# Scores of two attentions: the 64-row matmul with key lo runs over 128 rows, and key lo is loaded into both halves

## The chip, the cores and the metric

The kernel runs on one core of a Trainium2 chip. The metric is the device time of one execution in microseconds (us), median of three runs; lower is better. The engines are TensorE (PE in the rows, its weight loads PEld), VectorE (DVE), ScalarE (ACT), GpSimd (POOL) and SyncE (SP), which issues the DMAs.

## The reference, cut to what matters

Two blocks of two layers work on 512 tokens of 1024 features. Two of the mixers are attentions, and each computes scores with heads of 64 features:

```python
p1 = jax.nn.softmax(jnp.einsum('bqhd,bkhd->bhqk', q1, k1).astype(jnp.float32) * scale, axis=-1)
p2 = jax.nn.softmax(jnp.einsum('bqhd,bkhd->bhqk', q2, k2).astype(jnp.float32) * scale, axis=-1)
p = (p1 - lam * p2).astype(v.dtype)
...
s = jnp.einsum('bqgrd,bkgd->bgrqk', qg, k).astype(jnp.float32) * (d ** -0.5)
...
scores = jnp.einsum("bpnqhd,bpnkhd->bpnhqk", qb, kw) * (1.0 / math.sqrt(dh))
...
scores = jnp.where(valid[:, None], scores + bias, NEG_INF)
```

The first three lines are the differential heads of the first attention, the fourth its grouped heads (queries of 512 tokens, keys of 256 context tokens and of the 512), and the last two the second attention, with 16 heads, three dilated windows each and a bias by distance.

All of it is in fp32.

## The kernel before

Every fp32 operand of a product is split into two parts, hi and lo, in the matmul type fp32r; a general product takes three matmuls, hi by hi, hi by lo and lo by hi (`mm`, L187 to L192). A score uses that a head has only 64 features: `stack` (L707) puts q hi of head i of a pair into its own 64 rows of a tile and q lo into the other 64, and `load_twice` (L715) puts k hi into both halves of a tile. One matmul over 128 rows (L730) then gives (q hi + q lo) by k hi. A second one over the head's 64 rows (L731) adds q hi by k lo. Its k lo comes from `load_one` (L722), which loads a pair's two heads into one tile.

The first attention (`attention1`) has 48 blocks of 128 queries: four differential heads in two pairs, with two scores a block, and eight grouped heads with one, so 64 scores; a score has 768 keys, as 512 and 256 columns, and so two L730 and two L731. The second (`attention2`) has 64 blocks, eight pairs of heads with eight blocks each. A block has three scores, one of 512 keys (into bank `s0`) and two of 128 (into `s1`), so three L730 and three L731. Scores run two blocks ahead of the products with v. Between them `q_steps` weaves in the query products of the next pair (bank `side`). A block's softmax goes over DVE (L1414, L1417, L1426), ACT (L1422) and POOL, is transposed on PE (L825), split by ACT and DVE (L145, L148), and multiplied with v (L841).

PE takes its instructions in the written order inside the attentions; the other engines and the DMA issues are ordered by a scheduler at build time. All loads stand in one queue, SP's. `shift` and `accs` are two tiles of the layer norm (`ln_begin`, L498), in use until the norm ahead of the second attention is done and again in the norm behind it.

Of the kernel before, what the change touches and what calls it, by code (L numbers as in the profile page):

```python
# [15 lines left out]
PSUM = bass.MemoryType.PSUM  # L16
# [12 lines left out]
# PE takes its products in the order in which they are written  # L29
# [23 lines left out]
class Head:  # L53
    # the first products of the part behind a norm: the tokens that it ends first come first
# [27 lines left out]
class QueryHead(ColumnHead):  # L82
    # done before the attention's own banks are there
# [9 lines left out]
class TokenHead(Head):  # L93
    # 128 tokens by 512 columns to a bank, chunks of two row tiles
# [11 lines left out]
class Net:  # L106
# [26 lines left out]
    def side(self):  # L133
        # the bank of what is woven between the blocks of an attention
        return self.t(self.ps, [P, 512], F32, "side", 1)
# [37 lines left out]
    def chunk(self, name, idx, nb, w=128, k0=0):  # L173
# [4 lines left out]
        with ExitStack() as es:  # L178
            # behind the norm that the products before this one wait for
            if self.gated:  # L180
                self.gated -= 1
                for g in self.gate:
                    es.enter_context(self.tc.issue_after(g.ins))
            self.split(src, hi, lo)
# [14 lines left out]
    def out_gemm(self, names, base, xs, update, finish=None, tail=4, lead=0, loads=None, done=(0, 0)):  # L199
        # a product that adds to x; its last column tiles by halves of the tokens, for the norm behind it  # L200
        # done = (m, k): the first m column tiles have their first k row tiles in x already
# [8 lines left out]
        # the first column tiles at once, row tile by row tile: the last of them may still be in the making  # L210
# [14 lines left out]
        # x is updated behind the products of the next column tile  # L225
# [102 lines left out]
    def affine_split(self, t, a, b, hi, lo, R=None):  # L328
        # hi + lo = t * R * a + b
# [10 lines left out]
    def setup(self, es):  # L340
# [18 lines left out]
        # two regions of 16 tiles: what a product reads, and what is made from it  # L359
        self.rp = self.pool(es, "regions")  # L360

# [1 line left out]
    def ada_raw(self, pool, l, m, tag, bufs):  # L363
        # 128 columns of the modulation's weights, columns on the partitions
# [10 lines left out]
    def ada_start(self):  # L375
        # silu(c) and silu(c_ctx) along the rows of all partitions
# [11 lines left out]
    def ada_first(self, k):  # L388
        # shift and scale of row tile k of layer 0's mixer, for both conditions; the second sum is left to a later call
# [25 lines left out]
    def gain(self, l, which):  # L415
        # norm gain times (1 + scale)
# [5 lines left out]
    def ada_rest(self, l, j, engine=None):  # L422
        # column blocks of 512, 12 to a layer; summed over the partitions with a later call
# [54 lines left out]
    def rms_end(self, sl, a, b):  # L478
        # h = x * rsqrt(mean x^2 + eps) * a + b
# [23 lines left out]
    def ln_update(self, m, ps, scale, sl):  # L503
        # the sums run over x less the mean of its first 256 features: no more than 4 times the variance
# [116 lines left out]
    def gained(self, pool, ps, gain, tag, bufs, g=None, s=None):  # L621
        # ps * gain and ps ^ 2, out of PSUM
# [8 lines left out]
    def mean_sq(self, v, s, dim, eps, rhs=None):  # L631
        # column sums of s, as means and eps, into v
# [4 lines left out]
    def scaled_steps(self, g, y, gain=None):  # L637
        # g by the rows of y: [128 tokens, tiles of 128 tokens * groups of rows]
# [17 lines left out]
    def q_steps(self, next_chunk, dst, slot=None):  # L656
        # a column tile of queries, in steps; dst takes the rows for the scores, or what the norm goes on with
# [11 lines left out]
    def q_norm_steps(self, next_chunk, dsts, slots, v, key=None):  # L669
        # two column tiles of queries with their norms, and the keys'  # L670
# [18 lines left out]
    def diff_norm_steps(self, ots, zs):  # L689
        # the norms of the differential heads; zs has the sums of the first softmax  # L690
# [16 lines left out]
    def stack(self, q, src, view=lambda z: z):  # L707
        # head i of a pair as 128 rows: hi where src has it, lo in the other half
# [6 lines left out]
    def load_twice(self, pool, src, i, tag, bufs):  # L715
        # the rows of head i, in both halves
# [10 lines left out]
    def score(self, out, q, kk, kl, i, qs, ks):  # L727
        # (q hi + q lo) k hi + q hi k lo
        r = slice(64 * i, 64 * i + 64)
        self.nc.tensor.matmul(out=out, lhsT=q[i][:, qs], rhs=kk[:, ks], start=True, stop=False)  # L730
        self.nc.tensor.matmul(out=out, lhsT=q[i][r, qs], rhs=kl[r, ks], start=False, stop=True)  # L731
# [33 lines left out]
    def v_store(self, pool, vt, slot):  # L765
# [3 lines left out]
        # hi and lo of a head side by side, in the other order for the second one  # L769
# [6 lines left out]
    def v_all(self, pool):  # L776
        # the values of the four differential heads, tokens on the partitions: context, then latents
# [18 lines left out]
    def scores(self, q, k, i, qt):  # L796
        # [128 queries, 768 keys] of head i of a pair
# [5 lines left out]
    def softmax(self, pool, s):  # L803
        # exp(s - max) and its sums; what follows the maximum with a second call
# [12 lines left out]
    def p_t(self, e, pt, q, nk):  # L817
        # transposes P and splits it
# [17 lines left out]
    def pv_stacked(self, ps, v, pt, nk, i, out, parts=1):  # L836
        # (v hi + v lo) (p hi + p lo): those with v hi in the rows of head i, those with v lo in the others
# [11 lines left out]
    def diff_weights(self, ap, q, k, i, qt, zs, fill):  # L849
        # (softmax 1 - lam softmax 2) times the sum of softmax 1, which the norm of the head takes out  # L850
# [15 lines left out]
    def gqa_weights(self, ap, q, k, i, qt):  # L866
        # query heads m and m + 4 share a tile: the rows of head m + 4 i are those of key head i
# [8 lines left out]
    def lam(self):  # L876
        # misc[:, 0] = -(exp(lq1.lk1) - exp(lq2.lk2) + lam_init), misc[:, 1] = subln (1 - lam_init)
# [14 lines left out]
    def attention1_start(self, es, hc):  # L892
        # the first modulation and norm, and the queries of the differential heads and two tiles of keys with them:
        # row tile by row tile, as they come
# [5 lines left out]
        with self.tc.manual_schedule(engines=PE_ORDER):  # L900
# [10 lines left out]
            # products that take the row tiles as they come: queries, then keys  # L911
# [777 lines left out]
```

## Time and profile before

| what | value |
|---|---|
| median of 3 runs | 3589.59 us (3586.48 to 3591.5) |
| span of the profiled execution | 3579.7 us, 9.9 us below that median |
| PE busy | 3422.9 us, 96% of the span |
| weight loads (PEld) busy | 2843.5 us, 79% |
| DVE, ACT, POOL busy | 58%, 40%, 11% |
| granted clock of PE, mean | 0.976 of full speed |
| first attention, from its first score | about 188 to 446 us |
| second attention | about 2826 to 3138 us |

The span runs from the first to the last instruction of one execution that the profiler recorded; the profile gives no other time for that execution, and what lies around the span is taken as the difference to the median. Matmuls are pipelined and their recorded ends overlap, so what one costs is read from start to start.

### The profile page before, as it was taken

The page shows a single profiled execution, that of the slowest core. Times are in us where ns is not written, and L with a number is a line of the kernel's source. Part 1 is how long each engine was busy: PE and PEld are TensorE (multiplying, and loading weights), DVE is VectorE, ACT ScalarE, POOL GpSimd, SP SyncE. Part 2 cuts the span into 40 slices and gives each one's busy share as a digit, 9 for nine tenths or more (in the row PEclk, how much of TensorE's full clock was granted, in tenths as well). Part 3 has the DMA queues.
Part 4 walks back from the last instruction along what each step waited for, and adds up shares of the span by engine and source line. Part 5 has one row for each costly group of instructions (what it writes and reads, how often), then busy time and mean ns, then how long its engine had stood idle before and what let it go on. Part 6 is the DMA issues. An engine that isn't in the chain of part 4 may idle for free.

```text
span 3579.7 us, 43200 instructions
## 1 busy us (share of the span) xinstructions
PE 3422.9 (96%) x16646; PEld 2843.5 (79%) x16646; DVE 2068.3 (58%) x3471; ACT 1415.8 (40%) x2145; POOL 392.5 (11%) x391
## 2 busy tenths in 40 slices
PE   4888999999999999999999999999999999989998
PEld 3766688888888888888888888888888777778887
DVE  8766868776574555333766433453333777773335
ACT  4355643334443333222485422243222555552222
POOL 4023400000000000000313100110000321230001
PEclk9988999999999999999999999999999999999999
DMA  4641046542222222222222322245222122123221
GB/s 182 216 138 63 30 143 234 196 165 89 97 92 98 95 94 85 98 94 95 72 94 82 107 97 97 89 151 167 95 100 89 39 77 77 38 83 114 93 99 49
DMA packets 123775, 377.11 MB, mean 105 GB/s; under 512 B 13105, under 2 KB 27569, under 8 KB 123442
## 3 DMA queue, kind: packets, MB, share of 16 engines
q1 hardware_dynamic: 123426, 374.23, 30.6%
q8 instruction: 131, 2.15, 0.2%
q14 instruction: 74, 0.61, 0.0%
q10 hardware_dynamic: 144, 0.13, 0.0%
HBM read 355.95 MB, written 18.35 MB: 105 GB/s over the span
## 4 chain that ended last, share of the span: by engine, by line
PE 86%; DVE 8%; ACT 3%; issue 2%; DMA 1%; POOL 0%; SPq 0%; DVEq 0%; ACTq 0%; POOLq 0%
PE b L191 24%; PE b L192 24%; PE b L190 24%; PE side L190 2%; PE b L825 2%; PE s L731 2%; PE bo L841 2%; PE side L191 1%; PE side L192 1%; PE s L730 1%; PE b L731 1%; PE b L730 1%; DVE wl L148 1%; DVE x L515 1%; DVE acc L316 1%
## 5 line engine op out<-in xcount | busy, mean ns | idle before, releaser
L191 PE MATMUL b<-reg,wh 128*128 128x512 f32 (+1 forms) x4289 | 1573.2, 369 | 24.2 <-DVE reg L337 14.5
L190 PE MATMUL b<-reg,wh 128*128 128x512 f32 (+1 forms) x4289 | 1540.4, 369 | 33.8 <-ACT reg L336 11.7
L192 PE MATMUL b<-reg,wl 128*128 128x512 f32 (+1 forms) x4289 | 1569.2, 368 | 2.6 <-DVE wl L148 2.6
L145 ACT ACTIVATE wh<-raw 128x1024 fp32r<-128x1024 f32 (+3 forms) x550 | 561.1, 1026 | 1347.0 <-PE b L191 1178.0
L148 DVE TENSOR_TENSOR wl<-raw,wh 128x1024 fp32r<-128x1024 f32 (+3 forms) x550 | 655.9, 1199 | 572.8 <-ACT wh L145 561.4
L191 PEld LDWEIGHTS b<-reg,wh 128*128 128x128 f32 x4289 | 820.5, 191 | 159.6 <-DVE reg L337 16.6
L190 PEld LDWEIGHTS b<-reg,wh 128*128 128x128 f32 x4289 | 801.6, 191 | 170.7 <-ACT reg L336 13.7
L192 PEld LDWEIGHTS b<-reg,wl 128*128 128x128 f32 x4289 | 820.9, 191 | 133.9 <-DVE wl L148 4.0
L515 POOL TENSOR_TENSOR x<-x,shift 128x512 f32<-128x512 f32 x18 | 30.6, 1725 | 2388.2 <-ACT shift L513 2388.2
L592 DVE TENSOR_TENSOR sg<-sg,b 128x512 f32<-128x512 f32 x88 | 60.5, 687 | 284.4 <-PE b L192 283.8
L1524 DVE SCALAR_TENSOR_TENSOR x<-b,x 128x512 f32<-128x512 f32 x64 | 44.2, 691 | 190.3 <-PE b L192 190.3
L145 ACT ACTIVATE pth<-b 128x384 fp32r<-128x384 f32 (+1 forms) x160 | 82.3, 532 | 145.1 <-PE b L825 143.6
L315 ACT ACTIVATE sq<-x 128x256 f32<-128x256 f32 (+1 forms) x111 | 52.4, 473 | 176.7 <-DVE x L507 84.9
L148 DVE TENSOR_TENSOR ptl<-b,pth 128x384 fp32r<-128x384 f32 (+1 forms) x160 | 94.9, 607 | 35.4 <-ACT pth L145 33.5
L145 ACT ACTIVATE reg<-sg 128x512 fp32r<-128x512 f32 x132 | 83.3, 631 | 80.6 <-DVE sg L597 77.5
L190 PE MATMUL side<-reg,wh 128*128 128x512 f32 x221 | 104.4, 472 | 4.5 <-DVE hn L651 3.4
L148 DVE TENSOR_TENSOR reg<-sg,reg 128x512 fp32r<-128x512 f32 x132 | 90.5, 685 | 22.3 <-ACT reg L145 22.3
L825 PE MATMUL b<-ident,e 128*128 128x128 f32 x544 | 88.3, 294 | 13.3 <-DVE ptl L148 7.4
L825 PEld LDWEIGHTS b<-ident,e 128*128 128x128 f32 x544 | 67.8, 150 | 31.3 <-issue 9.5
L371 DVE CUSTOM_DVE_ANT_0 ada<-ada,silu_c,cols 128x1024 f32<-128x1024 f32 x70 | 86.8, 1279 | 10.0 <-DMA ada<-ada 9.9
L191 PE MATMUL side<-reg,wh 128*128 128x512 f32 x221 | 89.6, 406 | 0.0
L192 PE MATMUL side<-reg,wl 128*128 128x512 f32 x221 | 89.3, 404 | 0.0
(325 smaller groups left out, 3700.5 us busy)
## 6 DMA issues: line engine op xcount, KB each, us to landing
raw<-up SPq DMA_DIRECT2D x264, 512.0 KB, 3.3
ada<-ada SPq DMA_DIRECT2D x86, 512.0 KB, 4.5
raw<-down SPq DMA_DIRECT2D x96, 448.0 KB, 3.2
raw<-down SPq DMA_DIRECT2D x48, 512.0 KB, 3.3
raw<-q SPq DMA_DIRECT2D x24, 512.0 KB, 3.3
raw<-rg_in SPq DMA_DIRECT2D x20, 512.0 KB, 3.2
raw<-attn_in SPq DMA_DIRECT2D x14, 512.0 KB, 5.5
raw<-ada SPq DMA_DIRECT2D x10, 512.0 KB, 4.0
```

The costliest lines, as they stand in the source:

```text
L145: return self.nc.scalar.activation(out=hi, in_=src, func=AF.Copy, scale=scale)
L148: return self.nc.vector.tensor_tensor(out=lo, in0=src, in1=hi.bitcast(F32), op=ALU.subtract)
L190: mm(out=ps, lhsT=ah, rhs=bh, start=first, stop=False)
L191: mm(out=ps, lhsT=ah, rhs=bl, start=False, stop=False)
L192: mm(out=ps, lhsT=al, rhs=bh, start=False, stop=last)
L371: self.nc.vector.tensor_tensor_reduce(out=r, in0=r, in1=self.silu_c, scale=1.0, scalar=self.col("ada_b", 48 * l + m), op0=ALU.mult, op1=AL ...
L515: (nc.vector if k < 5 else nc.gpsimd).tensor_tensor(out=self.x[k], in0=self.x[k], in1=self.shift, op=ALU.subtract)
L592: nc.vector.tensor_tensor(out=sg, in0=sg, in1=bu, op=ALU.mult)
L730: self.nc.tensor.matmul(out=out, lhsT=q[i][:, qs], rhs=kk[:, ks], start=True, stop=False)
L731: self.nc.tensor.matmul(out=out, lhsT=q[i][r, qs], rhs=kl[r, ks], start=False, stop=True)
L825: nc.tensor.transpose(out=b[:, i * P:(i + 1) * P], in_=e[:, (k0 + i) * P:(k0 + i + 1) * P], identity=self.ident)
L841: nc.tensor.matmul(out=ps, lhsT=v[:, k, :], rhs=pt[z][:, k, :], start=k + z == 0, stop=k == nk - 1 and z == 1)
```

## The change

`score` gives the second matmul all 128 rows of q and of k lo, as the first has: it then adds (q hi + q lo) by k lo. For that k lo must stand in both halves, so it is loaded by `load_twice`, for each head by itself. In the first attention the tiles `kl` stay four, each now for one head and one softmax. In the second the k lo of pairs with an even number goes to two tiles `kl0` and `kl1` with one buffer each, and that of pairs with an odd number to the tiles of the norm, `accs` and `shift`.

```diff
     def score(self, out, q, kk, kl, i, qs, ks):
-        r = slice(64 * i, 64 * i + 64)
         self.nc.tensor.matmul(out=out, lhsT=q[i][:, qs], rhs=kk[:, ks], start=True, stop=False)
-        self.nc.tensor.matmul(out=out, lhsT=q[i][r, qs], rhs=kl[r, ks], start=False, stop=True)
+        self.nc.tensor.matmul(out=out, lhsT=q[i][:, qs], rhs=kl[:, ks], start=False, stop=True)
...
                 if m < 2:
                     src = self.kscr[2 * m:2 * m + 2]
-                    if i == 0:
-                        kl[m] = [self.load_one(inp, z[1], "kl", 4) for z in src]
-                    k[m, i] = [(self.load_twice(inp, z[0], i, "kk", 4), l) for z, l in zip(src, kl[m])]
+                    k[m, i] = [tuple(self.load_twice(inp, z[n], i, t, 4) for n, t in enumerate(("kk", "kl"))) for z in src]
...
                 elif m == 2 and i == 0:
-                    kl[2] = self.load_one(inp, self.kscr[4][1], "kl", 4)
                     for j in range(2):
-                        k[2, j] = (self.load_twice(inp, self.kscr[4][0], j, "kk", 4), kl[2])
+                        k[2, j] = tuple(self.load_twice(inp, self.kscr[4][n], j, t, 4) for n, t in enumerate(("kk", "kl")))
...
     def attention2_inputs(self, m):
-        k = [self.load_twice(ap, self.k2scr[m][0], 0, "kk0", 2), None, self.load_one(ap, self.k2scr[m][1], "kl", 2)]
-        if m == 0:
-            self.nc.sync.dma_start(out=self.tab, in_=self.a["dist"])
-        k[1] = self.load_twice(ap, self.k2scr[m][0], 1, "kk1", 2)
+        k = []
+        for i in range(2):
+            lo = (self.xp, ("accs", "shift")[i]) if m % 2 else (ap, f"kl{i}")
+            k.append((self.load_twice(ap, self.k2scr[m][0], i, f"kk{i}", 2), self.load_twice(lo[0], self.k2scr[m][1], i, lo[1], 1)))
+            if m + i == 0:
+                self.nc.sync.dma_start(out=self.tab, in_=self.a["dist"])
...
-                    self.score(out, q[g], k[i], k[2], i, qs, ks)
+                    self.score(out, q[g], k[i][0], k[i][1], i, qs, ks)
```

Three places show what the built programs make of it. On PE, this is one block of a pair with an odd number in the second attention, before (`kk` and `kl` hold key hi and key lo, `q` and `reg` queries):

```order
L192 MATMUL side_22951<-reg_2_3820_21401,wl_22948 128x512
L730 MATMUL s_4134_22974<-kk_4120_22931,q_4067_22671 128x512
L731 MATMUL s_4134_22974<-kl_22934,q_4067_22671 128x512
L730 MATMUL s_4135_22975<-kk_4120_22931,q_4092_22791 128x128
L731 MATMUL s_4135_22975<-kl_22934,q_4092_22791 128x128
L730 MATMUL s_4135_22975<-kk_4120_22931,reg_14_4114_22907 128x128
L731 MATMUL s_4135_22975<-kl_22934,reg_14_4114_22907 128x128
L190 MATMUL side_22951<-reg_3_3821_21402,wh_22947 128x512
```

The same place after the change, where source lines stand one lower:

```order
L192 MATMUL side_22987<-reg_2_3826_21425,wl_22984 128x512
L729 MATMUL s_4143_23010<-kk_4128_22963,q_4075_22703 128x512
L730 MATMUL s_4143_23010<-accs_22966,q_4075_22703 128x512
L729 MATMUL s_4144_23011<-kk_4128_22963,q_4100_22823 128x128
L730 MATMUL s_4144_23011<-accs_22966,q_4100_22823 128x128
L729 MATMUL s_4144_23011<-kk_4128_22963,reg_14_4122_22939 128x128
L730 MATMUL s_4144_23011<-accs_22966,reg_14_4122_22939 128x128
L190 MATMUL side_22987<-reg_3_3827_21426,wh_22983 128x512
```

The order is the same, and key lo of this pair now comes from `accs`. The size in a row is that of the output, so the 64 rows of the second matmul before don't show in it.

On SP, this is the start of the second attention, before (`raw` are the query weights):

```order
L159 DMA raw_21349<-q 128x1024
L159 DMA raw_21355<-q 128x1024
L159 DMA raw_21361<-q 128x1024
L159 DMA raw_21861<-q 128x1024
L159 DMA raw_21871<-q 128x1024
```

And after:

```order
L159 DMA raw_21373<-q 128x1024
L159 DMA raw_21379<-q 128x1024
L159 DMA raw_21385<-q 128x1024
L719 DMA shift_22198<-k2scr_9_64 64x512 x2
L719 DMA accs_22192<-k2scr_9_64 64x512 x2
L159 DMA raw_21885<-q 128x1024
L159 DMA raw_21895<-q 128x1024
```

The loads of the second pair's key lo into `shift` and `accs` now stand behind the third load of query weights and ahead of the fourth.

Also on SP, the loads for the third head of the first attention, before:

```order
L719 DMA kk_1787<-kscr_4_59 64x768 x2
L719 DMA kk_1790<-kscr_5_60 64x768 x2
L366 DMA raw_1933<-ada 128x1024
L159 DMA raw_2008<-attn_in 128x1024
L741 DMA vh_1793<-vscr_62 128x768
L741 DMA vl_1795<-vscr_62 128x768
```

And after:

```order
L719 DMA kk_1791<-kscr_4_59 64x768 x2
L719 DMA kl_1794<-kscr_4_59 64x768 x2
L719 DMA kk_1797<-kscr_5_60 64x768 x2
L719 DMA kl_1800<-kscr_5_60 64x768 x2
L366 DMA raw_1943<-ada 128x1024
L159 DMA raw_2018<-attn_in 128x1024
L740 DMA vh_1803<-vscr_62 128x768
L740 DMA vl_1805<-vscr_62 128x768
```

Key lo of this head was loaded ahead of these rows, with that of the head behind it; now its four loads stand among those of key hi, ahead of the next loads of weights.

## Rows read from the trace of the kernel before

**Rows 1.** The chain of waits, 2826 to 3138 us, shares by line.

```profile
by line: PE s L731 18.6%; PE side L190 18.0%; PE s L730 14.9%; PE side L191 14.0%; PE side L192 14.0%; PE bo L841 9.1%; PE b L825 8.5%; ACT wh L145 0.6%; issue 0.5%; DVE reg L148 0.4%; ACT e L1422 0.3%; DVE wl L148 0.3%; DVE e L1417 0.2%; D
```

**Rows 2.** Busy time by stretch: us, PE, PEld, DVE, ACT, POOL, clock, DMA share, GB/s.

```profile
188.00:331.00 143.00, 128.49 (x528) 89.64 (x526) 87.95 (x195) 74.51 (x142) 41.48 (x24) 0.81 0.27 90
331.00:446.00 115.00, 102.63 (x555) 77.62 (x556) 95.93 (x188) 69.75 (x153) 54.75 (x35) 0.91 0.12 42
2826.00:3138.00 312.00, 310.03 (x1439) 227.28 (x1439) 241.80 (x628) 160.16 (x292) 61.19 (x126) 0.99 0.19 65
```

**Rows 3.** Busy time by stretch, eight blocks of the second attention.

```profile
2869.95:2908.91 38.96, 38.96 (x185) 28.69 (x185) 30.68 (x80) 20.15 (x37) 7.69 (x16) 1.00 0.23 77
```

**Rows 4.** Timeline of PE, second attention: start us, us, line, output, inputs.

```profile
2999.82 0.39 PE L192 MATMUL side<-reg,wl 128*128 128x512 f32 x1
3000.05 0.40 PE L730 MATMUL s<-kk,reg 128*128 128x512 f32 x1
3000.38 0.49 PE L731 MATMUL s<-kl,reg 64*128 64x512 f32 x1
3000.80 0.33 PE L730 MATMUL s<-kk,reg 128*128 128x128 f32 x1
3001.05 0.32 PE L731 MATMUL s<-kl,reg 64*128 64x128 f32 x1
...
3001.82 0.50 PE L190 MATMUL side<-reg,wh 128*128 128x512 f32 x1
...
3002.39 0.40 PE L192 MATMUL side<-reg,wl 128*128 128x512 f32 x1
...
3009.80 0.39 PE L730 MATMUL s<-kk,reg 128*128 128x512 f32 x1
```

**Rows 5.** Timeline of the weight loads, same block.

```profile
3000.37 0.18 PEld L731 LDWEIGHTS s<-kl,reg 64*128 64x128 f32 x1 [0.36 <-issue]
...
3001.92 0.19 PEld L191 LDWEIGHTS side<-reg,wh 128*128 128x128 f32 x1
```

**Rows 6.** Timeline of PE in the gating unit, 128-column matmuls.

```profile
955.14 0.27 PE L192 MATMUL b<-wsh,v 128*128 128x128 f32 x1
...
960.84 0.27 PE L192 MATMUL b<-wsh,v 128*128 128x128 f32 x1
```

**Rows 7.** Instructions of L731: count, ns least, median, most, first and last start.

```profile
L731 PE MATMUL b<-kl,reg x128: 379/492/793, 189.0 to 441.2; 64*128 64x512 f32 x64, 64*128 64x256 f32 x64
...
L731 PE MATMUL s<-kl,reg x128: 322/325/502, 2826.9 to 3136.6; 64*128 64x128 f32 x96, 64*128 64x512 f32 x32
```

**Rows 8.** Timeline of PE, one score of the first attention.

```profile
420.27 0.28 PE L841 MATMUL bo<-ptl,vl 128*128 128x256 f32 x1
420.39 0.40 PE L730 MATMUL b<-kk,reg 128*128 128x512 f32 x1
420.71 0.50 PE L731 MATMUL b<-kl,reg 64*128 64x512 f32 x1
421.14 0.38 PE L730 MATMUL b<-kk,reg 128*128 128x256 f32 x1
421.45 0.38 PE L731 MATMUL b<-kl,reg 64*128 64x256 f32 x1
421.76 0.88 PE L825 MATMUL b<-ident,e 128*128 128x128 f32 x6
```

**Rows 9.** DMA issues on the page: count, KB each, us to landing.

```profile
raw<-q SPq DMA_DIRECT2D x24, 512.0 KB, 3.3
```

**Rows 10.** Last reads of accs, and ScalarE taking query weights.

```profile
L281 PE MATMUL norm<-ones,accs x8: 250/250/272, 2790.2 to 2799.3; 128*128 128x1 f32 x8
...
2825.83 2.01 ACT L145 ACTIVATE wh<-raw 128x1024 fp32r<-128x1024 f32 x2
```

**Rows 11.** Timeline of PE, query matmuls at the lower clock.

```profile
2830.01 0.63 PE L191 MATMUL side<-reg,wh 128*128 128x512 f32 x1
2830.43 0.63 PE L192 MATMUL side<-reg,wl 128*128 128x512 f32 x1
```

More of the change, by code (lines that the diff above doesn't have):

```diff
@@ L1020, in attention1 @@
             due = {j + AHEAD: j for j in range(len(blocks))}
-            q, k, kl, v, es_, pts = {j: [] for j in range(6)}, {}, {}, {}, {}, {}
+            q, k, v, es_, pts = {j: [] for j in range(6)}, {}, {}, {}, {}
             q[0], q[1] = [qs[0], qs[1]], [qs[2], qs[3]]
```

## The prediction

> **What bounds the kernel now.** I read the chain of waits first, in the second attention. It runs over TensorE (PE) nearly all the time, and the reader should see that the two matmul lines of a score, L731 and L730, hold 18.6% and 14.9% of it, the first of them more than any other line [rows 1]. Then I read the busy time by stretch. In the second attention (2826 to 3138 us) PE is busy 310.03 of 312 us at a granted clock of 0.99, so nothing but PE ends a wait there, and VectorE (DVE) has 241.80 us of work. The first attention is two stretches: in 188 to 331 us (differential heads) PE is busy 128.49 of 143 us and DVE 87.95, at a clock of 0.81; in 331 to 446 us (grouped heads) PE 102.63 of 115 and DVE 95.93 [rows 2]. Eight blocks in the steady middle of the second attention, one pair of heads, last 38.96 us, all of it PE, with 30.68 us of DVE [rows 3].
>
> Last I read PE instruction by instruction. Recorded durations overlap, so only the distance from start to start tells what a matmul costs. In one block of the second attention the row to see is how that distance jumps at each change between 128 rows and 64 rows. A 512-column matmul costs 0.23 us where its neighbours have 128 rows (2999.82 to 3000.05). The 512-column score pair costs 0.33 and 0.42 us, and the 128-column matmuls 0.25 each [rows 4]. The weight loads show why: the load for the 64-row matmul starts at 3000.37, when its matmul starts, not ahead of it, while between two 128-row matmuls the next load (3001.92) starts inside the matmul before it (3001.82) [rows 4, 5].
>
> **The change part by part.** *The score in the second attention.* From the first score matmul (3000.05) to the third query matmul behind the scores (3002.39) lie two 512-column and four 128-column score matmuls and two 512-column query matmuls: 2.34 us [rows 4]. With all of them over 128 rows I price 512 columns at 0.23, and 128 columns at the pace of another place in this kernel where 128-row, 128-column matmuls of the same type follow each other: 51 distances from 955.14 to 960.84, 0.112 us each [rows 6]. That is 4 x 0.23 + 4 x 0.112 = 1.37, so a block saves 0.97 us of PE. There are 64 blocks of three scores (the rows count the 128 second matmuls whose queries lie in the region tiles, the other 64 take their queries from elsewhere) [rows 7]. 64 x 0.97 = 62 us of PE time.
>
> Not all of it can be had. A block takes 4.875 us now (3000.05 to 3009.80 is two blocks) and PE would need 3.90 [rows 4]. DVE needs 30.68 / 8 = 3.835 us a block [rows 3], 98% of that. DVE runs its rows in order and some wait for ScalarE, so I let it be busy 95%, an estimate: 4.04 us a block, 0.835 saved, 64 x 0.835 = 53 us. The ends: 62 us if DVE keeps up with PE, and 33 us if it keeps half of its present idle time, (38.96 - 30.68) / 2 = 4.14 us in eight blocks, which gives (30.68 + 4.14) / 8 = 4.35 us.
>
> *The score in the first attention.* Here a score is a pair with 512 and a pair with 256 columns, 1.37 us from 420.39 to the transposes at 421.76, at full clock; at 0.23 and 0.12 (a 128-row matmul of 256 columns, 420.27 to 420.39) it would be 0.70 [rows 8]. That saves 0.67 for each of 64 scores [rows 7], 21.4 us in each of the two stretches, which have 32 scores each. In the first stretch DVE has only 62% of the time and PE 90%, but PE also stands still there for chains through DVE and ScalarE; I take 70%, 15 us. Ends: 8 us, if the chains take two thirds of it, and 26 us, since a mean clock of 0.81 means that 38% of the stretch ran at half clock, where each score saves up to twice as much (0.67 x 1.38 x 32 = 30; I stop below it). In the second stretch the whole 21.4 us would leave 93.6 us, less than the 95.93 us of DVE work [rows 2]; with DVE 95% busy it is 101 us, a saving of 14. I take 11, because the chains of a softmax stay; ends 5 and 17.
>
> *The loads of key lo.* Five loads become 20 of half the size in the first attention and eight become 32 in the second, about 4 MB more in all. In the first attention a head's keys are asked for one head ahead, and a head lasts 143 / 4 = 36 us [rows 2]; a 512 KB load, larger than any of these, lands in 3.3 us [rows 9]. They wait for the same buffers to come free as the loads of key hi just ahead of them in SyncE's queue, so the weight loads behind them wait no longer than they do now, but for the issues. I cost them at nothing; if the cover were gone it would be some microseconds at each of eight pairs.
>
> *The loads into the tiles of the layer norm.* The order shows the loads into `shift` and `accs` ahead of the fourth and fifth load of query weights, at the start of the second attention. They wait for the norm's last read of `accs`, on PE at 2799.3, and the weight loads wait behind them. ScalarE takes the weights at 2825.83 [rows 10]; from 2799.3 a few issues and 3.3 us of landing end well before that. Cost nothing, with some 20 us of cover. Before the first attention no more bytes are asked for than now: the four loads for the second head stand where the loads of the later heads' key lo stood.
>
> *What the scheduler moved.* The scores keep their places on PE; DVE's rows are reordered in the first attention, with none added. I price that at nothing and leave it to the ends of the two stretches.
>
> The sum: 53 + 15 + 11 = 79 us. The profiled execution has a span of 3579.7 us, and the median of the runs, 3589.59, stands 9.9 above it; I take that rim as unchanged. 3589.6 - 79 = 3511 us. The ends of the terms give 46 us (3544) and 105 us (3485).
>
> A rule that speaks against this: the row shows a 128-row weight load that starts 0.10 us into the 128-row matmul before it [rows 4, 5]. The Trainium skill, "TensorE: Matmul & The Clock Gate", Part 3, "Packing small matmuls", says that a weight load overlaps a matmul in flight only where the two use different row groups. By that rule full-row matmuls could not hide their loads, the 128-row scores would gain nothing, and the sum would be 3590. The trace doesn't agree, since the load at 3001.92 lies inside the matmul of 3001.82, and the sum goes by the row.
>
> **The rivals.** *DVE or ScalarE takes over early.* DVE keeps most of its waits, and each microsecond that PE gains is spent waiting for a softmax. For it: DVE at 79% now, in order, and 98% of the new PE pace [rows 3]. Against it: some of its idle time is waiting for these very scores. Gains from 7 to 46 us: 3544 to 3582.
>
> *More than the sum.* In the first attention the gaps vanish, the clock stays at its upper level and the first stretch saves more than 26 us. For it: the clock of 0.81 [rows 2]. Under 3485, perhaps 3475.
>
> *No change.* The distances in the score come from something other than the change of rows, such as two matmuls on one bank with the same weights. Against it: the query matmuls L190 and L191 also share bank and weights and run at the 0.23 pace away from a switch. The rule above would lead here too. 3590.
>
> *Slower.* PE, no longer the bound, gets gaps, and in the second attention TensorE's granted clock drops to the lower of its two levels (1.2 in place of 2.4 GHz). There a 512-column matmul takes 0.42 (2830.01 to 2830.43) [rows 11], 1.83 times as long; a block of 3.90 becomes 7.1 us, 3.1 more than the forecast's 4.04. It decides from 79 / 3.1 = 26 of the 64 blocks; with half of the blocks it is 3511 + 32 x 3.1 = 3610. For it: the first stretch, where PE is busy 90% and the clock 0.81. Against it: in the second stretch PE is busy 89% and the clock was 0.91, and the forecast leaves PE busy 3.90 / 4.04 = 97% [rows 2].
>
> **How the numbers follow.** Forecast 0.72 (own range 3485 to 3544), early takeover 0.14, more than the sum 0.06, no change 0.05, slower 0.03. The range that leaves out no more than 2 in 10 takes in the forecast and the upper half of the takeover: 3485 to 3562. A difference within 0.2% (7 us) can't be told from none here. Faster 0.72 + 0.14 + 0.06 = 0.92, same 0.05, slower 0.03.
>
> **What would show it.** Right: in a block of the second attention the distances are 0.23 and 0.11 throughout and the score's weight loads start ahead of their matmuls; eight blocks last 32 to 33 us with DVE busy about 95%; the attentions last about 231 us (now 258) and 259 us (now 312); the clock stays near 0.99 in the second. Wrong: distances of 0.33 and 0.42 still there (no change); eight blocks of 35 us and more with DVE waiting for ScalarE (takeover); PE waiting for weight loads at 2826 us (the loads into the norm's tiles); a clock under 0.9 in the second attention (slower).

## The result, and the profile after

The kernel after takes 3503.59 us (median of 4 runs, 3501.93 to 3504.56), beside 3588.03 for the kernel before in the runs taken with it: a ratio of 0.9765, 95% interval 0.9752 to 0.9777, 84.4 us less. The forecast was 3511 (3485 to 3562). The profiled execution has a span of 3501.6 us and took 3503.41.

Busy time by stretch of the kernel after answers to [rows 2, 3]: the first attention from its first score to its 33rd (differential heads) and on to its last (grouped heads), the second attention, and eight of its blocks. Columns: stretch and its length, busy PE, PEld, DVE, ACT, POOL, granted clock, DMA share, GB/s.

```profile
190.30:294.60 104.30, 83.77 (x476) 72.32 (x474) 77.08 (x170) 67.73 (x131) 35.73 (x21) 0.89 0.49 141
294.60:411.00 116.40, 90.13 (x573) 81.16 (x574) 102.03 (x206) 72.07 (x158) 55.87 (x36) 0.88 0.05 16
...
2800.00:3058.00 258.00, 252.64 (x1439) 215.27 (x1439) 233.13 (x630) 162.84 (x292) 60.92 (x126) 0.98 0.26 84
...
2866.90:2898.40 31.50, 31.50 (x185) 27.12 (x185) 29.33 (x80) 20.61 (x37) 7.75 (x16) 1.00 0.32 101
```

Cut at the same two scores, the first attention of before was 131.5 and 121.0 us long:

```profile
188.70:320.20 131.50, 117.86 (x476) 81.39 (x474) 80.50 (x174) 68.84 (x131) 36.90 (x21) 0.81 0.29 96
320.20:441.20 121.00, 108.73 (x574) 81.98 (x574) 100.22 (x204) 72.45 (x158) 56.92 (x36) 0.90 0.11 40
```

So the first stretch lost 27.2 us, the second 4.6, and the second attention 54.3 (first to last score matmul: 310.1 before, 255.8 after). The three make 86.1 us, 8.0 more than the spans differ by (78.1): the kernel after is 1.6 us longer ahead of its first score, 4.0 between the two attentions (2385.3 before, 2389.3 after) and 2.4 behind the second. Eight blocks take 31.5 us in place of 38.96, PE is still busy all of them, and DVE now 93%.

The timeline of PE after answers to [rows 8] (a score of the first attention) and [rows 4] (the scores of a block of the second); the first column is the start, and the distance between starts is the cost.

```profile
331.58 0.40 PE L729 MATMUL b<-kk,reg 128*128 128x512 f32 x1
331.81 0.40 PE L730 MATMUL b<-kl,reg 128*128 128x512 f32 x1
332.05 0.28 PE L729 MATMUL b<-kk,reg 128*128 128x256 f32 x1
332.16 0.28 PE L730 MATMUL b<-kl,reg 128*128 128x256 f32 x1
332.28 0.82 PE L824 MATMUL b<-ident,e 128*128 128x128 f32 x6
...
2969.49 0.39 PE L729 MATMUL s<-kk,q 128*128 128x512 f32 x1
2969.72 0.40 PE L730 MATMUL s<-shift,q 128*128 128x512 f32 x1
2969.96 0.22 PE L729 MATMUL s<-kk,q 128*128 128x128 f32 x1
2970.02 0.28 PE L730 MATMUL s<-shift,q 128*128 128x128 f32 x1
...
2970.35 0.44 PE L190 MATMUL side<-reg,wh 128*128 128x512 f32 x1
2970.63 0.40 PE L191 MATMUL side<-reg,wh 128*128 128x512 f32 x1
2970.86 0.40 PE L192 MATMUL side<-reg,wl 128*128 128x512 f32 x1
```

The reader should see 0.23 to 0.24 us for each 512-column score matmul, 0.70 for a score of the first attention (331.58 to 332.28), and 1.37 from the block's first score matmul to the third query matmul (2969.49 to 2970.86), as priced. Single distances still vary (0.06 behind the first 128-column matmul, 0.28 behind the first query matmul, 2970.35 to 2970.63); it is their sum that meets the price. The timeline of the weight loads of the same block answers to [rows 5]: the load for the second matmul (2969.49) starts with the first one, 0.23 us ahead of its own, where the load for the 64 rows started with its own matmul.

```profile
2969.49 0.19 PEld L730 LDWEIGHTS s<-shift,q 128*128 128x128 f32 x1
2969.72 0.19 PEld L729 LDWEIGHTS s<-kk,q 128*128 128x128 f32 x1
2969.96 0.19 PEld L730 LDWEIGHTS s<-shift,q 128*128 128x128 f32 x1
```

The chain of waits from 2800 to 3058 us answers to [rows 1]. Its first shares:

```profile
by line: PE side L190 13.7%; PE side L191 13.0%; PE side L192 12.7%; PE bo L840 9.5%; PE s L730 8.4%; PE b L824 8.4%; PE s L729 7.9%; issue 3.4%; DVE wl L148 3.1%; DVE e L1413 2.8%; DVE reg L148 2.5%; DVE ptl L148 2.4%; DVE q L148 2.1%; DMA
```

The two score lines had 33.5% of a longer stretch and have 16.3%; DVE rows, none above 0.4% before, now hold up to 3.1%. PE's waits in the first attention (188 to 412 us) have grown; the columns are what waited for what, us in all, times, longest:

```profile
PE b L729 <- ACT e L811: 13.4, 4, 7.3
PE b L824 <- DVE ptl L148: 11.3, 13, 2.2
PE side L649 <- DVE spread L643: 8.9, 3, 5.4
```

In the first attention of before these three were 4.2, 6.5 and 4.5 us.

### The profile page after: what moved, and what is told of

The parts are those of the page before. It is cut to its first block, busy times and chain, and to the rows that moved or that the text cites. A ratio compares the mean times of both kernels' runs of the same rounds, so it can differ in the third digit from the quotient of the medians.

```text
span 3501.6 us, 43277 instructions
## 1 busy us (share of the span) xinstructions
PE 3319.6 (95%) x16646; PEld 2828.9 (81%) x16646; DVE 2059.7 (59%) x3471; ACT 1417.4 (40%) x2145; POOL 391.0 (11%) x391
## 4 chain that ended last, share of the span: by engine, by line
PE 82%; DVE 10%; ACT 3%; issue 2%; DMA 2%; POOL 0%; SPq 0%; ACTq 0%; DVEq 0%; POOLq 0%
PE b L191 25%; PE b L192 24%; PE b L190 24%; PE side L190 1%; PE bo L840 1%; PE side L191 1%; PE side L192 1%; PE b L824 1%; DVE wl L148 1%; DVE ptl L148 1%; DVE nm L806 1%; DVE x L515 1%; DVE reg L148 1%; PE s L730 1%; PE s L729 1%
## 5 line engine op out<-in xcount | busy, mean ns | idle before, releaser
L190 PE MATMUL b<-reg,wh 128*128 128x512 f32 (+1 forms) x4289 | 1546.7, 370 | 34.9 <-ACT reg L336 10.3
L824 PE MATMUL b<-ident,e 128*128 128x128 f32 x544 | 85.1, 287 | 23.5 <-DVE ptl L148 12.2
L371 DVE CUSTOM_DVE_ANT_0 ada<-ada,silu_c,cols 128x1024 f32<-128x1024 f32 x70 | 86.9, 1281 | 11.4 <-DMA ada<-ada 11.3
L316 DVE TENSOR_TENSOR acc<-acc,sq 128x256 f32<-128x256 f32 (+1 forms) x118 | 73.2, 621 | 26.9 <-ACT sq L315 25.5
```

The lines of the kernel that those rows point to most:

```text
L190: mm(out=ps, lhsT=ah, rhs=bh, start=first, stop=False)
L316: nc.vector.tensor_tensor(out=acc, in0=acc, in1=s, op=ALU.add)
L371: self.nc.vector.tensor_tensor_reduce(out=r, in0=r, in1=self.silu_c, scale=1.0, scalar=self.col("ada_b", 48 * l + m), op0=ALU.mult, op1=AL ...
L824: nc.tensor.transpose(out=b[:, i * P:(i + 1) * P], in_=e[:, (k0 + i) * P:(k0 + i + 1) * P], identity=self.ident)
```

## The experiments

All ratios are to the kernel before, run on the same chip. "First stretch" and "second stretch" are cut at the first, the 33rd and the last score, as above.

**The 64 rows again, in the kernel after.** Loads, tiles and the order on SyncE are those of the kernel after, and so is PE's order in the attentions. VectorE's and ScalarE's orders, which the scheduler makes anew, differ from it in 56 and 25 places of the first attention.

```diff
-        self.nc.tensor.matmul(out=out, lhsT=q[i][:, qs], rhs=kl[:, ks], start=False, stop=True)
+        r = slice(64 * i, 64 * i + 64)
+        self.nc.tensor.matmul(out=out, lhsT=q[i][r, qs], rhs=kl[r, ks], start=False, stop=True)
```

> Loads, tiles and the order on SyncE's queue are those of the kernel after; only the second matmul of each score runs over the head's 64 rows again. Theory (the switches between 128 and 64 rows cost the time): the whole gain goes, 3588 us within 7, and in the second attention the distances of 0.33, 0.42 and 0.25 us are back. Rival (the loads, the tiles of key lo or the order that the scheduler made of them brought the gain): about 3504. In between: each microsecond under 3588 is what the loads and the order give.

Measured: 3587.47 us, ratio 1.0005 (0.9992 to 1.0017). In the second attention the median distances are 0.319, 0.428, 0.257 and 0.254 us again. So the loads, the two tiles of the norm and the order on SyncE are together worth nothing that the interval (3 us less to 6 us more) lets one see, and the gain belongs to the rows of the second matmul. What the new order of VectorE and ScalarE is worth in the first attention, this run doesn't set apart; in the second attention the next run does, since it has the orders of before on PE, VectorE, ScalarE and GpSimd throughout.

**Each attention alone.** In the first run the scores of the first attention take `score` of before, here called `half_score`, and its loads; in the second run those of the second attention do.

```diff
-            self.score(s[:, o // 512, 0:n], q, k[0], k[1], i, slice(qt * P, qt * P + P), slice(o, o + n))
+            self.half_score(s[:, o // 512, 0:n], q, k[0], k[1], i, slice(qt * P, qt * P + P), slice(o, o + n))
...
-                    self.score(out, q[g], k[i][0], k[i][1], i, qs, ks)
+                    self.half_score(out, q[g], k[i], k[2], i, qs, ks)
...
```

> 128 rows in the second attention alone; the first attention has loads and scores of the kernel before. The trace of after gives the second attention 54.5 us, of which 52 to 53 are left at the end. Theory (two gains independent of each other): 3588 - 53 = 3535 us, ratio 0.985. Rival (the gain of the first attention comes later, through other clock or weight loads, and the second's is larger than its own stretch shows): under 3525. Rival (the clock takes part of it when the first attention runs longer): over 3545.

> 128 rows in the first attention alone; the second has loads and scores of the kernel before. The trace of after shows 30 us at the end of the first attention, of which 25 are left ahead of the second. Theory: 3588 - 25 to 30 = 3558 to 3563 us, and the first stretch (differential heads) some 27 us shorter, where 15 were predicted. If the 27 us come from the lower clock that before shows from 225 to 292 us and after doesn't, the windows of this run show the same higher clock there; if its clock is as low as before's and the stretch is shorter all the same, the size has another cause. Prediction's own sizes: 3588 - 26 = 3562.

Measured: the second attention alone 3536.19 us, 0.985 (0.9833 to 0.9867), 51.3 us less; the first alone 3553.98, 0.9903 (0.9889 to 0.9918), 33.5 us less. Together 84.8, which is the whole gain: as far as the intervals tell, the two don't depend on each other. The first attention gave more than the 25 to 30 us expected. Cut into the two stretches, the profiled executions show where (from the busy time by stretch of each; a gap is length less busy PE):

| run | score over | first: length | PE busy | clock | second: length | PE busy | clock |
|---|---|---|---|---|---|---|---|
| before | 64 rows | 131.5 | 117.86 | 0.81 | 121.0 | 108.73 | 0.90 |
| 64 rows again | 64 | 128.4 | 113.11 | 0.85 | 120.3 | 105.99 | 0.91 |
| second attention only | 64 | 135.4 | 122.17 | 0.77 | 125.4 | 113.49 | 0.85 |
| two switches (below) | 64 | 135.0 | 121.78 | 0.79 | 122.0 | 108.98 | 0.89 |
| after | 128 | 104.3 | 83.77 | 0.89 | 116.4 | 90.13 | 0.88 |
| first attention only | 128 | 105.0 | 84.85 | 0.87 | 116.4 | 90.26 | 0.88 |

With the same scores, the first stretch is the longer the lower its granted clock. The two runs that have the first attention of before to the letter were 8.3 and 4.5 us longer in both stretches together than the profiled execution of before.

One difference doesn't go with the rows. From the last score matmul of the first attention to the first of the second it is 2389.3 to 2389.5 us in the three kernels of the table that load the first attention's key lo as after does (64 rows again, after, first attention only), and 2385.3 to 2385.4 us in the three that load it as before. Those loads, or the orders that come with them, cost 4.0 us there; by what way stays open.

**Two switches in a block in place of six.** The kernel before, with the matmuls of a block of the second attention in another order. Rows and work stay the same; `outs` holds the same banks and keys, group by group, and `r` the 64 rows.

```diff
-                for g in range(3):
-                    ks = slice(0, 512) if g == 0 else qs
-                    out = s0 if g == 0 else s1[:, (g - 1) * P:g * P]
-                    self.score(out, q[g], k[i], k[2], i, qs, ks)
...
+                for g, lo, first in ((0, 0, 1), (1, 0, 1), (0, 1, 0), (1, 1, 0), (2, 1, 1), (2, 0, 0)):
+                    a, b = (q[g][i][r, qs], k[2][r, outs[g][1]]) if lo else (q[g][i][:, qs], k[i][:, outs[g][1]])
+                    nc.tensor.matmul(out=outs[g][0], lhsT=a, rhs=b, start=bool(first), stop=not first)
```

> The kernel before, with the six score matmuls of a block of the second attention in another order: 128 rows (512 columns), 128 rows (128), then the three over 64 rows, then the last over 128 rows. Two changes of the row count a block in place of six; no matmul is added or gets more rows. Theory (switches): three 64-row matmuls in a row run at 0.23 and 0.11 us, a block loses 0.69 of its 0.97 us, 64 blocks 44 us of PE, DVE lets nearly all of it through: 3544 to 3552. Rival (a 64-row matmul is slow wherever it stands, its weight load always late): distances of 0.42 and 0.25 between 64-row matmuls too, 3575 to 3588.

Measured: 3549.43 us, 0.9887 (0.987 to 0.9905), 38 us less, with a pair of heads at 33.5 us where it was 38.96. The timeline of PE in this run:

```profile
3000.80 0.45 PE L1412 MATMUL s<-kk,q 128*128 128x512 f32 x2
3001.17 0.56 PE L1412 MATMUL s<-kl,q 64*128 64x512 f32 x2
3001.57 0.27 PE L1412 MATMUL s<-kl,reg 64*128 64x128 f32 x1
3001.78 0.33 PE L1412 MATMUL s<-kk,reg 128*128 128x128 f32 x1
...
3002.45 0.40 PE L192 MATMUL side<-reg,wl 128*128 128x512 f32 x1
```

From the first score matmul to the third query matmul it is 1.65 us (2.34 before, 1.37 after), so the order alone saves 0.69, as expected: the four switches that went cost 0.17 each, and the two that are left 0.28, 0.14 each. The three 64-row matmuls take 0.61 us together (3001.17 to 3001.78) with a switch at their end, near the 0.23 + 0.11 + 0.11 of full rows plus one switch. A 64-row matmul is therefore not slow; the change of rows next to it is. The timeline of the weight loads in the same place:

```profile
3001.17 0.29 PEld L1412 LDWEIGHTS s<-kl,q 64*128 64x128 f32 x2 [0.18 <-issue]
3001.52 0.18 PEld L1412 LDWEIGHTS s<-kl,reg 64*128 64x128 f32 x1
3001.77 0.19 PEld L1412 LDWEIGHTS s<-kk,reg 128*128 128x128 f32 x1
```

At both switches the load starts with its own matmul (3001.17 and 3001.77), while that of the third 64-row matmul starts 0.05 us ahead of it (3001.52, matmul 3001.57). So the late load goes with the change of rows too, not with the 64 rows. The Trainium skill, "TensorEngine Tiling (Array Packing)", Key Properties, says that changing the tiling mode, not just the tile, drains TensorE. This run agrees as to the loss, 0.14 to 0.17 us a change; the drain itself stands in no row.

**More work for VectorE.** One more DVE instruction in each block of the second attention, on columns of `e` that nothing reads any more.

```diff
                 nc.vector.tensor_scalar(out=e[:, 0:512], in0=e[:, 0:512], scalar1=z[:, 1:2], scalar2=None, op0=ALU.mult)
+                nc.vector.tensor_scalar(out=e[:, 512:768], in0=e[:, 512:768], scalar1=z[:, 1:2], scalar2=None, op0=ALU.mult)
```

> The kernel after with one more VectorE instruction in each of the 64 blocks of the second attention: the 256 columns of e behind the first 512, which nothing reads any more there, are scaled as the 512 are, about 0.28 us by half of that row's 0.48. VectorE's 29.33 us in eight blocks become about 31.5, and PE's 31.50 stay. Prediction's estimate (VectorE can't be busy more than 95%): eight blocks last 33.2 us, 13 us in all, 3516. Rival (VectorE can be filled nearly to the end as long as its work stands ready; PE stays the bound): eight blocks of 31.5 to 32.0, 3503 to 3508. A third outcome, over 34 us for eight blocks, would say that VectorE had been the bound already.

Measured: 3516.53 us, 0.9794 (0.978 to 0.9809), 12.9 us above the kernel after. Busy time by stretch over sixteen blocks of this run:

```profile
2839.00:2904.60 65.60, 63.10 (x369) 54.21 (x368) 61.83 (x175) 40.54 (x73) 14.72 (x32) 1.00 0.30 97
```

Eight blocks take 32.8 us with DVE busy 94% and PE 96%: DVE stops short of full, as the prediction had put it at 95%. The added instruction took 0.347 us, 2.8 in eight blocks, and 1.3 of them came out as time. (The five steady pairs of this run last 32.3 to 35.0 us, 33.2 on average, which is what was expected.) So PE bounds the second attention of after, with VectorE close behind.

**Splits at the end of the second attention.** In after, the pair from block 48 on takes 35.4 us in place of 31.5, and PE waits there for DVE, which splits six finished tiles in blocks 55 and 56. Two kernels split about one tile a block, with the lo part on GpSimd (below) or on DVE, and the first products with the output weights take each tile once it is split.

```diff
...
-                    for j in {55: (0, 1, 2), 56: (3, 4, 5), 59: (6,)}.get(n, ()):
-                        self.split(o[j], hn[0][j], hn[1][j])
+                    for j in {55: (0, 1), 56: (2,), 57: (3,), 58: (4,), 59: (5,), 60: (6,)}.get(n, ()):
+                        self.hi(hn[0][j], o[j])
+                        nc.gpsimd.tensor_tensor(out=hn[1][j], in0=o[j], in1=hn[0][j].bitcast(F32), op=ALU.subtract)
+                        ready[0] += 1
```

> The kernel after; at the end of the second attention the splits of finished heads go one to a block (blocks 55 to 60) with their lo on GpSimd, and the first products with the output weights take the tiles as they come. Theory (the 3.8 us that the pair from block 48 on loses against the 31.5 us of the steady pairs are VectorE's, which makes three lo tiles in block 55 and three in 56): that pair lasts about 32 us, PE's wait for VectorE's e of 5.1 us goes, 3498 to 3501 us. Rival (GpSimd's long subtractions slow VectorE or come late to the products): the pair gains nothing or the last one gets longer, 3503 to 3508.

> As the run before, with the lo of those splits on VectorE as in the kernel after. Theory (VectorE's whole work in the last eleven blocks is the bound, not that six splits stand in two blocks): the wait is spread over more blocks and no more than 2 us are won, 3501 to 3505. Rival (it is the bunching): the pair from block 48 on lasts about 32 us, 3498 to 3501.

Measured: 3502.25 and 3505.02 us, ratios 0.9757 (0.9743 to 0.9772) and 0.9763 (0.9747 to 0.978), no change from after. The pair from block 48 on lasts 38.2 and 36.2 us, the last one 26.7 and 27.5 (35.4 and 27.8 in after). My reading was wrong: the two last pairs of after take 63.2 us together, two steady ones 63.0, so nothing was there to be won; what the first of the two loses, the last gives back. In the kernel after run again the two take 34.4 and 28.9 us, 63.3 together.

**The new waits in the first attention.** First the transposes of the head norms come later in PE's order; then the grouped heads' scale goes from GpSimd to ScalarE; then both. The kernel after was run again beside the last two.

```diff
-        for _ in range(7):
+        for _ in range(12):
...
-        for _ in range(7):
+        for _ in range(16):
...
-            self.nc.gpsimd.tensor_tensor(out=e, in0=e, in1=r.to_broadcast([P, 768]), op=ALU.mult)
+            self.nc.scalar.activation(out=e, in_=e, func=AF.Copy, scale=r)
```

> The kernel after, with the transposes of the head norms of the first attention put later in PE's order (12 and 16 steps behind the reciprocal root in place of 7). Theory (the second stretch gave back part of its gain since PE, faster now, stands at a transpose before VectorE has its input): PE's waits for spread fall from 8.9 us (longest 5.4) to under 3, and the time to 3494 to 3500 us. Rival (VectorE, busy 87% from 296 to 416 us, bounds that stretch): the wait turns up in another row, most likely a transpose of the softmax behind VectorE's ptl, and the time stays at 3501 to 3506.

> The kernel after unchanged, beside the next two, so that differences of some microseconds can be told: 3502 to 3505 us, the second stretch of the first attention 116 to 117 us.

> The kernel after, with the grouped heads' e scaled by the reciprocal on ScalarE in place of GpSimd (32 instructions of 128x768, 1.47 us each there). In the trace of after, VectorE's instructions that read no PSUM take up to 1.98 us in place of 0.42 when GpSimd works, 10 us more in all in the second stretch; those that read PSUM take no longer. Theory (the second stretch gained less than predicted since VectorE is the bound there, in part through GpSimd): VectorE's excess falls from 10 to under 3 us, and the stretch from 116 to 107 to 112 us; total 3494 to 3500. Rival (ScalarE, 71 us busy in 116, gets 30 us more and now bounds the chain of a softmax): the stretch as long or longer, total 3502 to 3512.

> Both edits: the scale on ScalarE and the transposes of the head norms later in PE's order. If VectorE's excess and PE's waits for spread each cost time of their own: 3490 to 3497 us. If the stretch has one bound that neither touches: 3499 to 3505, as the runs with one edit.

| run | us | ratio | first stretch | its clock | second stretch |
|---|---|---|---|---|---|
| after again | 3503.60 | 0.9764 (0.975 to 0.9777) | 104.3 | 0.89 | 116.4 |
| later steps | 3499.35 | 0.9751 (0.9736 to 0.9765) | 99.1 | 0.93 | 117.7 |
| scale on ScalarE | 3500.57 | 0.9757 (0.9744 to 0.9771) | 105.6 | 0.87 | 112.6 |
| both | 3493.80 | 0.9739 (0.9726 to 0.9753) | 97.5 | 0.96 | 112.3 |

PE's waits from 188 to 412 us with later steps alone:

```profile
PE b L824 <- DVE ptl L148: 17.9, 20, 3.7
PE b L729 <- ACT e L811: 13.6, 7, 5.6
PE side L649 <- DVE spread L643: 2.7, 3, 1.5
```

The wait for `spread` goes from 8.9 to 2.7 us, and that for `ptl` rises from 11.3 to 17.9, so the second stretch is no shorter: the rival held there. The first stretch is 5.2 us shorter, where I had not looked for it, but in part by the cut: PE has 7 instructions fewer in it and 10 more in the second. The two together last 216.8 us, 3.9 less than in after. The whole kernel doesn't show it clearly: the interval overlaps that of after, and the profiled execution (3504.53 us) was no shorter than that of after. The scale on ScalarE takes 3.8 us from the second stretch, a little less than the 4 to 9 expected, and its time lies between the two ranges that were named. Busy time of that stretch with the scale on ScalarE:

```profile
293.90:406.50 112.60, 88.95 (x573) 78.55 (x574) 92.87 (x206) 96.28 (x188) 8.22 (x6) 0.91 0.05 17
```

DVE has 9.2 us less to do than in after and the stretch is 3.8 shorter, with DVE at 82%. So DVE's total is not the bound of that stretch; PE still stands 17 to 19 us behind `ptl`, the chain of transpose, ScalarE and DVE. What would shorten it stays open. Both edits together give 3493.8 us, 9.8 below the kernel after on the same chip by the medians, though the two intervals touch. That lies inside the 3490 to 3497 expected if each of the two costs time of its own.

## Why the prediction was right, step by step

- **The switch of rows costs PE, 0.97 us a block.** Right, and shown by three runs: the gain goes when the 64 rows come back, two thirds of the switches give 0.69 us a block, and a block of after measures the 1.37 us. The late weight load, which the prediction gave as the reason, goes with the switch and not with the 64 rows.
- **Second attention, 53 us.** Right: 54.3 by the traces, 51.3 by the run of its own. The working was a little off on both sides. Eight blocks take 31.5 us, not 32 to 33, since DVE's recorded work fell from 30.68 to 29.33 us [rows 3] and so left PE the bound at 93%; and the blocks at both ends gave less than the steady ones (first pair 41.6 to 34.9, the last two 73.7 to 63.2). That DVE can't be filled beyond about 95% was an estimate, and the run with more work for DVE bears it out.
- **First attention, first stretch, 15 us with ends 8 and 26.** The term that was mis-sized: 27.2 us (24.1 to 31.1 against the four executions with 64 rows). "I take 70%" failed. PE's busy time fell by 34.1 us, which is 21.4 of matmuls at the upper clock and some 13 more, as the clock went from 0.81 to 0.89; gaps took back only 6.9 (13.6 before, 20.5 after). The pieces of the stretch at the lower level (granted clock 0.50), summed, before and then after:

```profile
sum 51.20, PE 43.85 PEld 30.71 DVE 34.11 ACT 23.18 POOL 16.14; mean PE 8.77 PEld 6.14 DVE 6.82 ACT 4.64 POOL 3.23
sum 23.91, PE 15.53 PEld 12.90 DVE 15.00 ACT 12.48 POOL 9.67; mean PE 3.88 PEld 3.22 DVE 3.75 ACT 3.12 POOL 2.42
```

By the 1.83 of [rows 11], an estimate, the 43.85 us of PE work there cost 19.9 more than they would at the upper level, and the 15.53 cost 7.0. Taken off, 98.0 us of PE work are left before and 76.7 after, some 21 apart. The other three executions with 64 rows come to 97.9 to 98.8 in the same way, the run with the first attention alone to 76.8. So 21.4 us was right for the work, and the rest is that the lower level held for 27 us less; why it did, no run shows. The factor of 1.38 for the lower clock, which the prediction worked out and stopped below, was the better guide.

- **First attention, second stretch, 11 us with ends 5 and 17.** Mis-sized the other way: 4.6 us by the two traces (3.9 to 9.0 against the four executions with 64 rows). PE's busy time fell by 18.6 us, and gaps grew from 12.3 to 26.3. "With DVE 95% busy it is 101 us" was no fit guide: DVE is at 88%. PE's waits of this stretch in after:

```profile
PE b L824 <- DVE ptl L148: 11.3, 13, 2.2
PE side L649 <- DVE spread L643: 5.9, 2, 5.4
PE b L824 <- POOL e L861: 2.8, 1, 2.8
```

Of the 14.0 us that the gaps grew, the chains of a softmax, which I had given 3 us, take 6.9 in two rows (`ptl` from 6.5, GpSimd's `e` from 0.7). The wait for `spread`, of the head norms, was not there in this stretch before and stands in no term of the prediction; it takes 5.9.

- **The sum.** The first attention was put at 26 us and gave 31.8 by the traces, with both its terms outside their own ends: misses of 12.2 us too low and 6.4 too high, which partly cancel. The 8.0 us by which the rest of the kernel grew, put at nothing, take off more than is left. That the spans differ by 78.1 us beside a forecast of 79 is in part luck; that of the second attention is not.
- **Loads at nothing, the norm's tiles too.** Right within what the medians tell: 1.0005 (0.9992 to 1.0017) with all loads in place and 64 rows. It isn't right to the microsecond, since the 4.0 us between the attentions go with the first attention's loads or their orders. At the norm's tiles nothing was lost: PE waits 3.9 us for ScalarE ahead of the second attention's first score, before and after. The rows of the matmuls that read the norm's tiles, with busy time, mean ns and idle time ahead:

```profile
L730 PE MATMUL s<-shift,q 128*128 128x512 f32 (+1 forms) x32 | 9.1, 335 | 0.0
L730 PE MATMUL s<-accs,q 128*128 128x512 f32 (+1 forms) x32 | 9.1, 336 | 0.0
```

- **The rim of 9.9 us, "taken as unchanged".** A misreading. In the twelve other profiled executions, whose own time is known, time and span differ by 1.7 to 1.8 us. So the profiled execution of before took about 3581.5 us, near the shortest of its executions (3580.49 to 3593.48). The two runs with the same first attention spent 260.8 and 257.0 us there, beside 252.5 in this execution, so the difference probably lies in that part; before itself was profiled only once. That is why the medians show 84.4 us and the spans 78.1, beside a forecast of 79.
- **The rivals.** Early takeover by DVE would have shown eight blocks of 35 us and more; PE was busy all of 31.5. The clock in the second attention stayed at 0.98, so the slower case had no ground. No change is excluded by the result: the distances fell while the banks, the query tiles and PE's order in the attentions stayed. More than the sum came true in its number for the first stretch, 27.2 us, but not in its condition: the gaps grew there, and the clock rose only to 0.89.

## What to carry to other kernels

A matmul over fewer rows than its neighbours is no saving: each change of the row count cost 0.14 to 0.17 us in the second attention here, so half-height operands are better stacked or doubled up to the full 128 rows, or at least put next to each other. Where a part of a stretch runs at the lower clock, size a saving of PE work by the clock of that part, not by the upper one: here 21 us of matmuls gave 34 us of PE's busy time. Where an in-order PE waits for chains through two other engines, as in the grouped heads, most of what it saves can turn into longer gaps (14.0 of 18.6 us there).

## What the runs showed of the hardware

GpSimd held up VectorE, and only some of its instructions. Timeline of DVE in the kernel after, then of POOL (start, us):

```profile
331.41 0.16 DVE L272 TENSOR_TENSOR rsq_b<-dn_y 128x16 f32<-128x16 f32 x1
...
332.59 1.25 DVE L272 TENSOR_TENSOR rsq_b<-dn_y 128x16 f32<-128x16 f32 x1
...
338.32 0.96 DVE L272 TENSOR_TENSOR rsq_b<-dn_y 128x16 f32<-128x16 f32 x1
```

```profile
332.34 1.47 POOL L871 TENSOR_TENSOR e<-e,rz 128x768 f32<-128x768 f32 x1 [1.34 <-DVE dn_y L274]
336.89 2.36 POOL L871 TENSOR_TENSOR e<-e,rz 128x768 f32<-128x768 f32 x1 [3.08 <-DVE rz L812]
```

The same 16-column instruction takes 0.16 us alone, and 1.25 and 0.96 when it meets GpSimd's; both of the long ones end 0.03 us behind GpSimd's end (333.84 and 333.81, 339.28 and 339.25). VectorE's instructions that read PSUM (`ptl`, `nm`) keep their 0.55 and 0.95 us beside GpSimd. The Trainium skill, "SBUF — State Buffer", "SBUF: two separate sides", says that the two engines share a port pair as an exclusive lock, which a VectorE instruction with two SBUF inputs needs too, and that whichever starts first has it for its whole instruction while the other is blocked. These rows agree. In the second stretch it added some 10 us to VectorE's work, and with the scale on ScalarE some 2.

Also unexpected: with work standing ready, VectorE's recorded busy time for the same instructions is less (30.68 to 29.33 us in eight blocks), since the record of each starts before that of the one ahead has ended (in the kernel after one starts at 330.95 and lasts 0.55, and the next starts at 331.41); a busy share of before therefore overstates a little what an engine will need once its gaps close.
